# Down projection of a hybrid decoder layer: one block of weights loaded later, from another queue

## The chip, the cores and the metric
The kernel runs on one core of one Trainium2 chip. The metric is the device time of one execution in microseconds (us); the median of three timed executions stands for a kernel. A separate execution is recorded by the hardware profiler, and its trace gives every row below.

The engines are named as the profile names them: PE (TensorE, the matrix engine), PEld (its weight loads), DVE (VectorE), ACT (ScalarE), POOL (GpSimd) and SP (SyncE, which here only issues DMAs). Each engine works through its own instructions in order and waits at one until what it needs is there. DMAs are issued by SP, by POOL or by ACT; "SPq" and "POOLq" are the issues in the profile.

## The reference
One decoder layer in float32 on 512 tokens of width 1024: RMSNorm, attention heads of two kinds, an output projection, then RMSNorm, SwiGLU and a last RMSNorm with a gain:

```
h = h + mix @ w_out
hn = rms_norm(h, norm2_g)
h = h + (silu(hn @ w_gate) * (hn @ w_up)) @ w_down      # w_down: 2816 x 1024
return rms_norm(h, norm_f_g)
```

The change touches only how the product with `w_down` gets its weights.

## The kernel before
All matrix products are made in three passes on a high and a low part of each operand, so that float32 accuracy is kept: `hi*hi + hi*lo + lo*hi`. For each operand ACT makes the high part (a cast, line 70) and DVE the low part (a subtraction, line 75).

**The stages.** Attention and the output projection come first, then the SwiGLU units (22 units of 128 hidden columns), and at the end the down projection, from about 545 us on. The stage before it leaves the hidden activations `zs` in SBUF.

**The down projection** multiplies (512 x 2816) by (2816 x 1024). Rows of tokens, hidden columns and output columns are each cut in half, which gives blocks A11 to A22 of activations and B11 to B22 of weights, and the eight block products are replaced by seven products of sums of blocks (Strassen's scheme in Winograd's form). Here `rows_w(kh, ch, ...)` names a block of weights: kh = 1 is the lower half, ch = 1 the right half. Each product runs over 11 tiles of 128 hidden rows, taken in pairs: six steps, the last with one tile. So there are 42 steps (`steps`, line 909), numbered (n, k) in the code with n from 0; the text counts products from one, so the third product is n = 2.

One step (lines 935 to 955) does the following in order:
- `prepare(n, k)`: the activations are split by ACT (`xe`) and DVE (`xf`), then the weights by ACT (`hl`) and DVE (`hl`, which the profile also writes `hl<-raw,hl`). The split weights have three buffers, the activations four.
- the functions in the fifth field of the product's row in `products`. They change the blocks in place for a later product: `s1` to `s4` change activations on DVE, `t2` and `t3` change weights, and `add_w(kh, ch)` adds a block of weights from DRAM to B11 by accumulating DMAs that POOL issues (line 859).
- `multiply`: for each of two row halves and each tile three matmuls of 512 columns (lines 928 to 930), 12 in a full step, 66 in a product.
- after the third step of a product, the result of the product before is taken from PSUM and added to the output cells in SBUF (`evict`), and after the fourth step `close` squares finished cells on ACT and multiplies those of the left half by the gain `gf` on DVE (`gain`, line 887).

The order of DVE, ACT, POOL and PE within these steps is as written (`tc.manual_schedule`, line 933). The order of SP's loads is written out too (line 823): B11 and B21 (left half), the residual `h1d` into the cells, B22, B12, and last the two halves of `gf`. Outside such blocks a planner orders the instructions by simulated times.

**Where the blocks lie.** B21 takes over buffers that held the transposed input of the SwiGLU units (`x0`), and half of a `raw2` tile; it is read only by the second product. B12 has tiles of its own (`w_hl` and one `w_raw`). In `products` (line 901) the rows that use them are:

```
(ps_b, A12, B21, True, (s1,), ...),               # second product
(ps_a, A21, B11, False, (s4, add_w(1, 0)), ...),  # fourth
(ps_c, A12, B22, False, (t3,), ...),              # fifth
(ps_a, A11, B12, False, (), ...),                 # sixth
(ps_b, A22, B11, True, (), [], [])]               # seventh
```

`t3` adds B22 to B12 before the sixth product reads it. `add_w(1, 0)` in the fourth product adds the lower left block to B11, which the seventh product reads.

Of the kernel before, what the change touches and what calls it, by code (L numbers as in the profile page):

```python
# [11 lines left out]
F32 = mybir.dt.float32  # L12
F32R = mybir.dt.float32r
AF = mybir.ActivationFunctionType
ALU = mybir.AluOpType

P = 128
# [15 lines left out]
WC = 512  # L33
# [4 lines left out]
BUFS = {"w_raw": 3, "w_hl": 5, "pf": 2, "P": 2, "T": 2, "mf": 1, "oc": 1, "g": 3, "h1": 4, "pair": 1, "raw2": 6, "hl2": 3, "xe": 4, "xf": 4}  # L38
# [13 lines left out]
def tile_hybrid_layer(ctx: ExitStack, tc: tile.TileContext, xT, w_qk0, w_t, w_av, w_vb, w_o, w_gu, w_d,  # L52
                      rel, pos2, cw1, cb1, cw2, gT, gf_row, oh, cmask, out):
    nc = tc.nc
# [3 lines left out]
    ws = ctx.enter_context(tc.tile_pool(name="ws", bufs=2))  # L58
# [4 lines left out]
    def bank(tag):  # L63
        return psum.tile([P, 512], F32, name=tag, bufs=BANKS[tag])
# [9 lines left out]
    def tt(e, out, in0, in1, op):  # L74
        engines[e].tensor_tensor(out=out, in0=in0, in1=in1, op=op)  # L75
# [465 lines left out]
    for step in PLAN.split():  # L541
        n, i = step[0], step[1:]
# [34 lines left out]
    def raw2():  # L577
        return ff.tile([P, 2, WC], F32, name="raw2", bufs=BUFS["raw2"])
# [9 lines left out]
    def raw1():  # L588
        return ws.tile([P, WC], F32, name="w_raw", bufs=BUFS["w_raw"])
# [205 lines left out]
    def hidden(half, rows):  # L795

        v = []
        for k in PAIRS:
            j = k.start + (NJ - 10 if k.start < 10 else 1) * rows
            v.append(zq[min(j // 4, 4)][:, j - 4 * min(j // 4, 4):][:, :k.stop - k.start, half * HS:(half + 1) * HS])  # L800
        return v

    A11, A12, A21, A22 = [hidden(h, r) for h in range(2) for r in range(2)]

    def rows_w(kh, ch, n, i):
        k = PAIRS[n].start
        r = k + i + ((NJ - 10 if k < 10 else 1) if kh else 0)
        return w_d[r * P:(r + 1) * P, ch * HD:(ch + 1) * HD]

    def load_w(dst, kh, ch):  # L810
        for n, k in enumerate(PAIRS):
            for i in range(k.stop - k.start):
                nc.sync.dma_start(dst[n][:, i], rows_w(kh, ch, n, i))
# [4 lines left out]
    ps_a, ps_c, ps_b = [[bank(n) for n in tags] for tags in (("PT", "O"), ("S", "S"), ("proj", "proj"))]  # L818
# [4 lines left out]
    with tc.manual_schedule(engines={mybir.EngineType.SP}):  # L823
        r11 = [raw2() for _ in PAIRS]
        B11 = r11[:5] + [r11[5][:, 0:1]]
        load_w(B11, 0, 0)
        x0 = [ff.tile([P, n, WC], F32, name=tag, bufs=1)
              for n, tag in ((4, "X10"), (4, "X11"), (10, "X20"), (10, "X21"))]
        B21 = [x0[k // 2][:, 2 * (k % 2):2 * (k % 2) + 2] for k in range(4)] + [x0[2][:, 8:10], r11[5][:, 1:2]]
        load_w(B21, 1, 0)  # L830
        for t in range(NT):
            nc.sync.dma_start(x0[2][:, 2 * t:2 * t + 2], h1d[t].rearrange("p (c n) -> p c n", c=2))
        B22 = [x0[3][:, 2 * k:2 * k + 2] for k in range(5)] + [raw1()[:, None]]
        load_w(B22, 1, 1)
        B12 = [ws.tile([P, 2, WC], F32, name="w_hl", bufs=BUFS["w_hl"]) for _ in range(5)] + [raw1()[:, None]]
        load_w(B12, 0, 1)
        gf = [ff.tile([P, HD], F32, name="g", bufs=BUFS["g"]) for _ in range(2)]
        for c in range(2):
            nc.sync.dma_start(gf[c], gf_row[:, c * HD:(c + 1) * HD].to_broadcast([P, HD]))
# [16 lines left out]
    def add_w(kh, ch):  # L856
        def f(k):
            for i in range(B11[k].shape[1]):
                nc.gpsimd.dma_start(B11[k][:, i], rows_w(kh, ch, k, i), accum_op=ALU.add)  # L859
        return f  # L860

    def t2(k):
        if k < 4:
            add_w(1, 1)(k)
        else:
            tt("v", B11[k], B11[k], B22[k], ALU.add)

    def t3(k):
        tt("v", B12[k], B12[k], B22[k], ALU.add)

    def evict(ps, th, c, sign=1):

# [21 lines left out]
    def store(t):  # L894
# [7 lines left out]
        (ps_a, A11, B11, True, (s3, add_w(0, 1)), [(ps_a, 0, 0)], []),  # L902
        (ps_b, A12, B21, True, (s1,), [(ps_b, 0, 0)], [(0, 0), (1, 0)]),
        (ps_c, A21, B11, True, (s2, t2), [(ps_c, 1, 1)], []),
        (ps_a, A21, B11, False, (s4, add_w(1, 0)), [(ps_a, 0, 1, -1)], []),
        (ps_c, A12, B22, False, (t3,), [(ps_c, 0, 1)], [(0, 1), (1, 1)]),
        (ps_a, A11, B12, False, (), [(ps_a, 1, 1, -1), (ps_a, 1, 0)], [(2, 1), (3, 1)]),
        (ps_b, A22, B11, True, (), [], [])]
    steps = [(n, k) for n in range(7) for k in range(len(PAIRS))]

# [152 lines left out]
```

## Time and profile before
| | us |
|---|---|
| median of three timed executions | 665.92 (665.73 to 667.33) |
| the profiled execution | 669.47 |
| its span | 667.6 |
| PE busy | 628.0 (94%) |
| DVE busy | 530.5 (79%) |
| ACT busy | 379.5 (57%) |
| POOL busy | 170.0 (25%) |

The span runs from the first to the last instruction of the trace, and the profiled execution's time holds some 2 us around it. Shares of busy time are averages over all stages. A busy PE is not a PE at its peak: matmuls overlap, and their ends are modelled, so their starts are the safer reading.

### The profile page before, as it was taken

The numbers are of one execution on the slowest core, as the hardware profiler recorded it, in microseconds if no ns is written. First come the engines' busy times: TensorE is split into PE (matmuls) and PEld (weight loads), VectorE is DVE, ScalarE is ACT, GpSimd is POOL, SyncE is SP. The second block draws the span as 40 slices with busy tenths as digits, with TensorE's granted clock in tenths as the row PEclk, the third lists the DMA queues.
The fourth block names the chain that finished last, engine by engine and source line by source line (L and its number), as shares of the span: only waits on it lengthen the run. The fifth ranks groups of instructions, "written<-read, shape, count | busy, mean of one in ns | idle before, by whom it ended". The sixth has DMA issues, their size and how long they took to land.

```text
span 667.6 us, 11272 instructions
## 1 busy us (share of the span) xinstructions
PE 628.0 (94%) x3876; PEld 560.3 (84%) x3876; DVE 530.5 (79%) x1072; ACT 379.5 (57%) x785; POOL 170.0 (25%) x214
## 2 busy tenths in 40 slices
PE   9999997989999999987899999999999999859995
PEld 6878887868878888767799999999999988748784
DVE  4558867567787768649899989989999779669995
ACT  4553566245684668747864555555555636615572
POOL 6635852063445555430000000000000040414000
PEclk9999999979999999989899999999999999969998
DMA  5766576346415651043543333233233499949011
GB/s 178 211 189 188 168 182 165 100 132 164 130 36 172 187 192 33 1 163 106 189 141 102 108 127 122 87 111 109 97 113 108 164 258 322 305 85 160 1 63 63
DMA packets 52803, 92.29 MB, mean 138 GB/s; under 512 B 7643, under 2 KB 10971, under 8 KB 52748
## 3 DMA queue, kind: packets, MB, share of 16 engines
q1 hardware_dynamic: 47852, 82.68, 39.3%
q0 software_dynamic: 4320, 7.87, 6.8%
q10 hardware_dynamic: 576, 1.05, 0.4%
q8 instruction: 30, 0.49, 0.3%
q14 instruction: 25, 0.20, 0.1%
HBM read 76.32 MB, written 7.64 MB: 126 GB/s over the span
## 4 chain that ended last, share of the span: by engine, by line
PE 70%; DMA 11%; DVE 9%; ACT 5%; issue 3%; SPq 1%; POOL 1%; ACTq 0%; DVEq 0%; POOLq 0%
PE proj L88 8%; PE proj L90 8%; PE proj L89 8%; PE S L88 6%; PE S L89 6%; PE S L90 6%; PE PT L339 3%; DMA g<-in_gf_dram 2%; DMA X<-h1d 2%; PE S L316 2%; PE O L355 2%; PE O L358 2%; PE S L317 2%; DMA w_raw<-in_w_t_dram 1%; DMA X<-in_w_d_dram 1%
## 5 line engine op out<-in xcount | busy, mean ns | idle before, releaser
L859 POOL DMA_DIRECT2D raw<-in_w_d_dram x30 | 26.5, 1041 | 287.8 <-DVE hl L75 280.8
L70 ACT CAST hl<-raw 128x1024 fp32r<-128x1024 f32 (+1 forms) x69 | 70.5, 1022 | 40.5 <-PE S L930 16.7
L75 DVE TENSOR_TENSOR hl<-raw,hl 128x1024 fp32r<-128x1024 f32 (+1 forms) x69 | 81.2, 1178 | 3.0 <-ACT hl L70 2.9
L70 ACT CAST w_hl<-w_raw 128x512 fp32r<-128x512 f32 (+2 forms) x76 | 43.3, 576 | 63.6 <-PE S L90 19.2
L83 POOL TENSOR_TENSOR w_hl<-w_raw,w_hl 128x512 fp32r<-128x512 f32 (+1 forms) x47 | 61.2, 1306 | 65.2 <-ACT w_hl L70 26.2
L336 POOL TENSOR_SCALAR P<-P,den 128x512 f32<-128x512 f32 (+1 forms) x96 | 51.1, 551 | 39.9 <-DVE den L328 28.1
L324 ACT ACTIVATE P<-P,mn 128x512 f32<-128x512 f32 (+1 forms) x96 | 53.5, 558 | 11.8 <-DVE mn L322 11.5
L75 DVE TENSOR_TENSOR PTl<-PT,PTh 128x512 fp32r<-128x512 f32 (+2 forms) x96 | 43.8, 482 | 10.2 <-ACT PTh L349 9.7
L349 ACT CAST PTh<-PT 128x512 fp32r<-128x512 f32 (+2 forms) x96 | 38.1, 426 | 22.7 <-PE PT L339 18.8
L88 PE MATMUL S<-X,w_hl 128*128 128x256 f32 x176 | 49.9, 284 | 1.0 <-DVE h1t L75 0.5
L88 PE MATMUL S<-X,hl 128*128 128x256 f32 x176 | 50.0, 284 | 0.7 <-ACT xf L724 0.7
L322 DVE CUSTOM_DVE_ANT_0 P<-S,T 128x512 f32<-128x512 f32 (+1 forms) x96 | 43.9, 483 | 8.2 <-PE S L317 6.7
L89 PE MATMUL S<-X,hl 128*128 128x256 f32 x176 | 50.0, 284 | 0.3 <-DVE X L75 0.3
L89 PE MATMUL S<-X,w_hl 128*128 128x256 f32 x176 | 49.8, 283 | 0.0
L90 PE MATMUL S<-X,hl 128*128 128x256 f32 x176 | 49.7, 282 | 0.0
L90 PE MATMUL S<-X,w_hl 128*128 128x256 f32 x176 | 49.6, 283 | 0.0
L88 PE MATMUL proj<-xh,w_hl 128*128 128x512 f32 x112 | 46.1, 412 | 1.2 <-DVE va L281 1.1
L70 ACT CAST w_hl<-raw 128x512 fp32r<-128x512 f32 x45 | 27.3, 620 | 32.3 <-PE S L90 25.7
L90 PE MATMUL proj<-xh,w_hl 128*128 128x512 f32 x112 | 45.6, 407 | 0.0
L89 PE MATMUL proj<-xl,w_hl 128*128 128x512 f32 x112 | 45.4, 406 | 0.0
L83 DVE TENSOR_TENSOR w_hl<-w_raw,w_hl 128x512 fp32r<-128x512 f32 (+1 forms) x37 | 26.1, 710 | 15.0 <-ACT w_hl L70 14.9
L339 PE MATMUL PT<-ident,P 128*128 128x128 f32 x240 | 36.1, 273 | 0.8 <-POOL P L336 0.8
(305 smaller groups left out, 2047.5 us busy)
## 6 DMA issues: line engine op xcount, KB each, us to landing
raw<-in_w_gu_dram SPq DMA_DIRECT2D x46, 256.0 KB, 3.3
w_raw<-in_w_gu_dram SPq DMA_DIRECT2D x42, 256.0 KB, 2.7
raw<-in_w_d_dram POOLq DMA_DIRECT2D x30, 256.0 KB, 8.1
w_raw<-in_w_t_dram SPq DMA_DIRECT2D x28, 256.0 KB, 3.1
X<-in_w_d_dram SPq DMA_DIRECT2D x20, 256.0 KB, 7.5
T<-gd SPq DMA_DIRECT2D x64, 64.0 KB, 2.0
w_raw<-in_w_o_dram SPq DMA_DIRECT2D x16, 256.0 KB, 3.0
raw<-in_w_d_dram SPq DMA_DIRECT2D x12, 256.0 KB, 3.8
```

Source lines behind the costliest of these rows:

```text
L70: nc.scalar.copy(out, in_)
L75: engines[e].tensor_tensor(out=out, in0=in0, in1=in1, op=op)
L83: engines[lo].tensor_tensor(out=w[:, 1, :n], in0=raw[:, :n], in1=w[:, 0, :n].bitcast(F32), op=ALU.subtract)
L88: nc.tensor.matmul(ps, w[:, 0, sl], xh, start=first, stop=False, skip_group_check=skip)
L89: nc.tensor.matmul(ps, w[:, 0, sl], xl, start=False, stop=False, skip_group_check=skip)
L90: nc.tensor.matmul(ps, w[:, 1, sl], xh, start=False, stop=last, skip_group_check=skip)
L322: nc.vector.tensor_tensor_reduce(out=pp, in0=sv, in1=T[:, S - w:], op0=ALU.add, op1=ALU.min, scale=1.0, scalar=3e38, accum_out=mn[:, t:t + 1])
L324: nc.scalar.activation(pp, pp, AF.Exp, bias=mn[:, t:t + 1], scale=-1.0, accum_out=den[:, t:t + 1])
L336: nc.gpsimd.tensor_scalar(pp, pp, den[:, t:t + 1], 1.0, op0=ALU.mult, op1=ALU.mult)
L339: nc.tensor.transpose(pv[:, kb * P:(kb + 1) * P], pp[:, kb * P:(kb + 1) * P], ident)
L349: nc.scalar.copy(ov[0], pv)
L859: nc.gpsimd.dma_start(B11[k][:, i], rows_w(kh, ch, k, i), accum_op=ALU.add)
```

## The change
The upper right block is no longer loaded by SP into tiles of its own. In the fourth product POOL loads it (plain DMAs, the new function `load_12`) over B21, which the second product has read by then. `t3` and the sixth product use B21 in place of B12. The accumulating loads of the lower left block move from the fourth to the fifth product.

```diff
         load_w(B22, 1, 1)
-        B12 = [ws.tile([P, 2, WC], F32, name="w_hl", bufs=BUFS["w_hl"]) for _ in range(5)] + [raw1()[:, None]]
-        load_w(B12, 0, 1)
         gf = [ff.tile([P, HD], F32, name="g", bufs=BUFS["g"]) for _ in range(2)]
...
+    def load_12(k):
+        for i in range(B21[k].shape[1]):
+            nc.gpsimd.dma_start(B21[k][:, i], rows_w(0, 1, k, i))
+
     def t3(k):
-        tt("v", B12[k], B12[k], B22[k], ALU.add)
+        tt("v", B21[k], B21[k], B22[k], ALU.add)
...
-        (ps_a, A21, B11, False, (s4, add_w(1, 0)), [(ps_a, 0, 1, -1)], []),
-        (ps_c, A12, B22, False, (t3,), [(ps_c, 0, 1)], [(0, 1), (1, 1)]),
-        (ps_a, A11, B12, False, (), [(ps_a, 1, 1, -1), (ps_a, 1, 0)], [(2, 1), (3, 1)]),
+        (ps_a, A21, B11, False, (s4, load_12), [(ps_a, 0, 1, -1)], []),
+        (ps_c, A12, B22, False, (t3, add_w(1, 0)), [(ps_c, 0, 1)], [(0, 1), (1, 1)]),
+        (ps_a, A11, B21, False, (), [(ps_a, 1, 1, -1), (ps_a, 1, 0)], [(2, 1), (3, 1)]),
```

## Rows read from the trace of the kernel before

**Rows 1.** The page's 40 equal slices of the span: PE's busy share, in tenths.

```profile
PE   9999997989999999987899999999999999859995
```

**Rows 2.** Waits, 545 to 668 us, then DVE's, 595 to 641: total, times, longest.

```profile
DVE X L75 <- DMA g<-in_gf_dram: 10.5, 1, 10.5
PE S L929 <- DVE hl L75: 10.0, 1, 10.0
...
DVE hl L75 <- ACT hl L70: 0.4, 2, 0.2
```

**Rows 3.** DVE in order of time: start, duration, line, out<-in, [idle before].

```profile
567.29 0.68 DVE L75 TENSOR_TENSOR xf<-act,xe 128x512 fp32r<-128x512 f32 x1
...
576.90 1.22 DVE L75 TENSOR_TENSOR hl<-raw,hl 128x1024 fp32r<-128x1024 f32 x1
...
589.20 1.29 DVE L75 TENSOR_TENSOR X<-X,g 128x512 f32<-128x512 f32 x2 [10.48 <-DMA g<-in_gf_dram]
...
612.11 1.22 DVE L75 TENSOR_TENSOR w_hl<-w_hl,X 128x1024 f32<-128x1024 f32 x1
...
627.59 0.68 DVE L75 TENSOR_TENSOR xf<-act,xe 128x512 fp32r<-128x512 f32 x1
```

**Rows 4.** PE in order of time: products three, six and seven.

```profile
570.97 0.39 PE L928 MATMUL S<-hl,xe 128*128 128x512 f32 x1
...
581.85 0.39 PE L928 MATMUL S<-hl,xe 128*128 128x512 f32 x1
592.28 0.80 PE L929 MATMUL S<-hl,xe 128*128 128x512 f32 x1 [10.04 <-DVE hl L75]
...
629.46 0.50 PE L929 MATMUL PT<-hl,xe 128*128 128x512 f32 x1
...
644.33 0.39 PE L928 MATMUL proj<-hl,xe 128*128 128x512 f32 x1
```

**Rows 5.** Stretches: us, busy PE, PEld, DVE, ACT, POOL; PEclk, DMA, GB/s.

```profile
592.28:597.57 5.29, 5.29 (x12) 4.13 (x13) 5.29 (x9) 0.19 (x1) 0.00 (x0) 0.50 0.00 0
597.88:621.92 24.04, 24.04 (x108) 19.90 (x106) 23.80 (x31) 14.26 (x20) 9.66 (x11) 1.00 0.73 121
```

**Rows 6.** SP's issues in order of time.

```profile
565.84 0.33 SPq L813 DMA_DIRECT2D w_raw<-in_w_d_dram  x1
566.51 6.43 SPq L813 DMA_DIRECT2D w_hl<-in_w_d_dram  x10
...
573.94 1.20 SPq L839 DMA_DIRECT2D g<-in_gf_dram  x2
```

**Rows 7.** DMA by stretch: 552-554, 566-568, 570-573.5, 574-576, 576-578, 596-598.

```profile
raw<-in_w_d_dram POOLq DMA_DIRECT2D x1, 256.0 KB, 13.8
...
q1 hardware_dynamic: 443, 0.81, 105.9%
w_hl<-in_w_d_dram SPq DMA_DIRECT2D x3, 256.0 KB, 5.4
...
w_hl<-in_w_d_dram SPq DMA_DIRECT2D x5, 256.0 KB, 9.5
...
g<-in_gf_dram SPq DMA_DIRECT2D x2, 256.0 KB, 15.7
...
q1 hardware_dynamic: 144, 0.26, 39.7%
...
raw<-in_w_d_dram POOLq DMA_DIRECT2D x1, 256.0 KB, 3.7
```

**Rows 8.** POOL's issues in order of time (duration of the group).

```profile
569.71 1.75 POOL L859 DMA_DIRECT2D raw<-in_w_d_dram  x2 [17.33 <-DVE hl L75]
...
578.42 1.75 POOL L859 DMA_DIRECT2D raw<-in_w_d_dram  x2 [1.74 <-DVE hl L75]
597.88 1.75 POOL L859 DMA_DIRECT2D raw<-in_w_d_dram  x2 [17.71 <-DVE hl L75]
...
608.55 2.65 POOL L859 DMA_DIRECT2D raw<-in_w_d_dram  x3 [0.59 <-DVE hl L75]
```

## The prediction

> **What bounds the kernel now.** I read the 40 slices first. TensorE (PE) is busy 9 tenths nearly everywhere, but slices 35 and 36 of the row (568 to 601 us) fall to 8 and 5 [rows 1]; slice 40 is the tail. This is the down projection, the only stage that the diff touches, so everything below is read there. The list of waits names the stop: VectorE (DVE) waits once, 10.5 us, for the final gain `gf` to be loaded, and PE waits once, 10.0 us, for DVE's `hl` [rows 2]. In DVE's order of time the instruction that waits is the multiplication by the gain (`gain`, line 887), which starts at 589.20 after work that ended at 578.72 [rows 3]. It stands in the fourth step of the third product, in front of `hl` of the fifth step, which PE's second matmul of that step needs: PE starts one matmul at 581.85 and the next at 592.28 [rows 4].
>
> Two things follow. First, PE's clock: after the stop, from 592.28 to 597.57, the granted clock was 0.50 (1.2 of 2.4 GHz), and in the stretch from 597.88 it was 1.00 [rows 5]. Second, DVE from the stop on has no slack: from 595 to 641 it waited 0.4 us in all [rows 2]. Its work for products three to five runs from 567.29 to 627.59, 60.3 us, less the stop of 10.48 49.8 us [rows 3]; PE needs 3 x 66 matmuls at 0.2267 us (10.88 us for 48 matmuls, 570.97 to 581.85 [rows 4]) = 44.9 us. So in these three products DVE and not PE sets the pace, and PE's share only looks full because short waits lie inside overlapped matmuls. From the second matmul of product six (629.46) to product seven (644.33) PE needs 14.87 us for 65 matmuls [rows 4], 0.229 each: PE paces there.
>
> Why is `gf` late? SP issues in order. The last load of the lower right weights is issued at 565.84, then come ten loads `w_hl` from 566.51 on and one more (B12, 256 KB each), and `gf` only at 573.94 [rows 6]. It needs 15.7 us to land, since by then the two queues share the engines: SP's moved 144 packets in 576 to 578, against 443 in 566 to 568 [rows 7]. POOL's accumulating loads of the same time (pairs from 569.71 to 580.17, first and last of four [rows 8]) are the other half.
>
> **The change part by part.**
> *Removed from SP: eleven loads, 2.8 MB.* `gf` moves up to the place of the first of them, 566.5. Landing: the three `w_hl` loads issued in 566 to 568 took 5.4 us, those issued from 570 to 573.5 9.5 us, and `gf` itself 15.7 [rows 7]. So it lands between 571.9 and 582.2. I take 5.4, the row of the same moment: what lies ahead in SP's queue is the same lower right block, and POOL issues its first pair only 3.2 us later. DVE would need `gf` when it ends at 578.72; even 9.5 us (576.0) is in time. At the far end the wait would be 582.2 - 578.7 = 3.5 us.
>
> *What this returns.* At 5.4 or 9.5 us the whole stop of 10.48 us goes. DVE's stream from 589.20 on has no hole until 629.4, so all of it moves up by 10.48, and the first `hl` of product six, which releases PE at 629.46, with it. From there PE paces as before, and the tail hangs on product seven. So the term is 10.5 us. PE's own account gives a ceiling only: its second matmul of the stopped step moves from 592.28 to 582.08, 10.2 us; it would also not lose the 12 matmuls at half clock (5.29 - 12 x 0.2267 = 2.6 us) nor the short waits, (644.33 - 592.28) - 215 x 0.2267 - 2.6 = 0.7 us: 13.5 us together. That cannot be had, as DVE needs 4.9 us more than PE in products three to five, and its lead is small: `hl` of the fourth step ends at 578.12, PE needs it at 581.85 - 12 x 0.2267 = 579.13, so 1.0 us. The time at half clock cost nothing before, because PE then waited less for DVE; that is why I do not add the 2.6. What is late next is DVE's `hl`, in short waits of PE that add up to some 49.8 - 44.9 - 1.0 = 3.9 us over products three to five.
>
> *Added to POOL: eleven plain loads `load_12` in the fourth product.* They wait only for the second product's reads of the same tiles, long done, and stand on POOL's queue behind the third product's accumulating loads, which end their issue at 580.17. A pair of issues takes 1.75 us, 0.88 each, so eleven take 9.6 us: 580.2 to 589.8 [rows 8]. No plain load from this queue is in the trace; the accumulating ones landed in 3.7 us with the engines free and 13.8 us with all queues full [rows 7]. The first pair lands between 585.6 and 595.7. Its reader `t3` starts at 612.11 on DVE [rows 3], with the shift at 601.6: hidden with 6 us to spare at the worst end, and later steps gain, as a step of these products takes DVE 49.8 / 18 = 2.8 us and a pair of issues 1.75. I take zero; DVE would pay each us beyond 601.6.
>
> *Moved one product later: the lower left accumulating loads (`add_w(1, 0)`).* Each waits for the reads of product four, as before, and is now also queued behind `load_12`. They were issued from 597.88 to 611.20 [rows 8]; with the shift product four's readers would free the first at 587.4, and POOL comes to it at 589.8. Eleven issues at 0.88 from there could end by 599.4, but the last is held by its reader, near 600.7. Landing at the worst 13.8 us gives 614.5; PE begins product seven at 644.33 [rows 4], with the shift 633.8, and its operands are prepared at most three steps (8 us) ahead, from 625.6. Hidden by 11 us. Nothing else is on POOL in this stage.
>
> *`t3` and the split read another tile.* Same engine, shape and kind of operands, another place in SBUF: 1.22 us for `t3`'s `w_hl<-w_hl,X`, and 1.22 for a split from `raw` [rows 3]. Zero; no row bounds it better, and 0.1 us on each of ten instructions would be 1 us either way. The third product's accumulating loads lose the competition of B12 and land sooner; their readers are not waiting now, so nothing is gained.
>
> *A rule against the change.* POOL issued a pair in 1.75 us at 597.88, as at 569.71 [rows 8], in a stretch in which DVE was busy 23.80 of 24.04 us [rows 5]. The Trainium skill, page "SBUF — State Buffer", section "SBUF: two separate sides", warns that a DMA issued from GpSimd can be starved of descriptors by some VectorE instructions. By that rule `load_12` would appear after DVE stops (the third rival); the rows do not show such a stop beside these instructions.
>
> *Sum.* The profiled execution took 669.47 us with a span of 667.6, 3.55 us above the median of the runs, 665.92. Taking 10.5 off each: span 657.1, profiled 659.0, median 655.4.
>
> **The rivals.**
> *`gf` still lands late (0.09).* For it: both queues share the engines, and it took 15.7 us before. Against it: what made it slow was B12 ahead and eight accumulating loads beside; the first is gone and the second begins later than the new issue. At 15.7 us the wait is 3.5 us, the gain 7.0 and the time 658.9. The Trainium skill, page "DMA: Bandwidth & Descriptors", section "Issuing engines are not separate DMA queues", says that a transfer gains nothing by another issuing engine; that would hold if `load_12` were in flight beside `gf`, but its turn comes at 580.2.
>
> *No change (0.05).* `gf` could be held at its issue by something other than B12, such as the release of its buffer; then it is issued near 574 and DVE waits as before: 665.9. For it: no row names what released that issue. Against: its buffers were last used by the SwiGLU units, which end before the third product. A different order drawn up by the planner in front of the stage could likewise give back some us; its stages are not in the diff, so I fold this in here.
>
> *Slower: `load_12` cannot be issued beside DVE (0.05).* Place: POOL from 580.2. If POOL could not write its transfers while DVE works, they would start when DVE stops at `t3`, 601.6; the first pair would then cost DVE 1.75 us of issue and 3.7 to 13.8 us of landing, 5.5 to 15.6 us. It turns the result from 10.5 us on, that is from a landing of 8.8 us; at the far end 15.6 - 10.5 = 5.1 us slower, 671.0; at the near end 660.4. Against it stand the eleven issues of 597.88 to 611.20 beside a full DVE.
>
> **How the numbers follow.** The forecast, stop gone and DVE pacing, has 0.81, the rivals 0.09, 0.05 and 0.05. Its own spread is from the ceiling (13.5 us, 652.4) to a `gf` that costs one to two us. The range goes from 652.4 to 659.5 and takes in the first rival, leaving out the rest. About 0.3% (2 us) is what a measurement can tell from no change. Faster: 0.81 + 0.09, less a little for a planner that gives it back, and a part of the third rival is still faster: 0.90. Same: 0.05. Slower: 0.05.
>
> **What would show it.** Right: `gf` issued near 566 and landed before 578; no DVE wait for it, or under 1 us; no 10 us hole in PE and no stretch at clock 0.50 in the third product; eleven POOL issues from about 580 to 590; no DVE wait at `t3`; product six's second matmul near 619, product seven near 634. Short PE waits for `hl` in products three and five show that DVE paces. Wrong: DVE waiting at line 887 for more than 3 us, at `t3`, or on ACT's split of the fourth or seventh product for an accumulating load; or a product seven that starts near 634 with a tail longer than 23 us.

## The result and the profile after

The change made the kernel faster, by about as much as forecast.

| | before | after |
|---|---|---|
| median, us | 666.62 | 657.03 (656.30 to 657.83, 4 runs) |
| ratio | 1 | 0.9849, 95% interval 0.9814 to 0.9883 |
| profiled execution, us | 669.47 | 657.83 |
| its span, us | 667.6 | 656.1 |

The ratio is a gain of 10.1 us (7.8 to 12.4) on 666.62; the forecast was 10.5, and 655.4 us for the median. The line numbers below are those of the changed kernel: `gf` is loaded in line 837, and the matmuls are lines 930 to 932.

First the order in time of SP, which answers to [rows 6] (columns as there).

```profile
563.82 0.33 SPq L813 DMA_DIRECT2D w_raw<-in_w_d_dram  x1
564.53 1.01 SPq L837 DMA_DIRECT2D g<-in_gf_dram  x2
```

`gf` now follows the last lower right load at once, 0.7 us later, where it stood 8.1 us later before. It lands in 5.3 us in place of 15.7, at a moment when SP's queue has the engines to itself (the DMA view of 564 to 566 us; first the queue's packets, then the issues; it answers to [rows 7]):

```profile
q1 hardware_dynamic: 445, 0.81, 105.4%
...
g<-in_gf_dram SPq DMA_DIRECT2D x2, 256.0 KB, 5.3
```

DVE's order of time shows what that gives: the first splits of product three, the gain, `t3` of the first step, and the splits at the start of the sixth product, as in [rows 3].

```profile
565.84 0.69 DVE L75 TENSOR_TENSOR xf<-act,xe 128x512 fp32r<-128x512 f32 x1
566.73 1.23 DVE L75 TENSOR_TENSOR hl<-raw,hl 128x1024 fp32r<-128x1024 f32 x1 [0.20 <-ACT hl L70]
...
576.59 0.69 DVE L846 SCALAR_TENSOR_TENSOR act<-h1t,act 128x512 f32<-128x512 f32 x1
577.19 1.29 DVE L75 TENSOR_TENSOR X<-X,g 128x512 f32<-128x512 f32 x2
...
599.77 1.22 DVE L75 TENSOR_TENSOR X<-X,X 128x1024 f32<-128x1024 f32 x1
...
615.26 0.69 DVE L75 TENSOR_TENSOR xf<-act,xe 128x512 fp32r<-128x512 f32 x1
615.86 1.22 DVE L75 TENSOR_TENSOR hl<-X,hl 128x1024 fp32r<-128x1024 f32 x1
```

The gain carries no idle time, and neither does `t3`. The gain starts 12.01 us earlier than in [rows 3]. Of that, 1.45 us is not the change's: this execution reached product three that much earlier (the split of the activations that starts it is at 565.84, at 567.29 in [rows 3]). In the profile of a kernel below that has the stop again, the down projection is reached earlier than before too (its first `hl` on DVE at 544.24, before 545.88, after 544.43). The rest, 10.56 us, is the stop. By product six the lead is 12.33 us, since a wait of 0.24 us for ACT at the fifth product's start went too. At the end of the span 11.5 us of it are left (667.6 against 656.1): from the start of DVE's last instruction to the end, which is the last stores, it took 5.7 us, 4.9 before. Without the earlier arrival the trace thus shows 10.1 us, as the times do. In the list of waits of DVE from 560 to 640 us one row is left, and PE's own list in the same stretch has two small ones in place of 10.0 us [rows 2]:

```profile
DVE hl L75 <- ACT hl L70: 1.6, 5, 0.7
```

```profile
PE PT L931 <- DVE hl L75: 0.8, 1, 0.8
PE S L931 <- DVE hl L75: 0.6, 1, 0.6
```

PE's order of time shows where these are: the second matmul of products four and six, and one in product five ([rows 4] has the stop and product six).

```profile
584.48 0.39 PE L930 MATMUL PT<-hl,xe 128*128 128x512 f32 x1
585.63 0.49 PE L931 MATMUL PT<-hl,xe 128*128 128x512 f32 x1 [0.76 <-DVE hl L75]
...
608.83 0.39 PE L930 MATMUL S<-hl,xe 128*128 128x512 f32 x1
609.86 0.50 PE L931 MATMUL S<-hl,xe 128*128 128x512 f32 x1 [0.64 <-DVE hl L75]
...
616.71 0.39 PE L930 MATMUL PT<-hl,xe 128*128 128x512 f32 x1
617.14 0.50 PE L931 MATMUL PT<-hl,xe 128*128 128x512 f32 x1
...
632.00 0.39 PE L930 MATMUL proj<-hl,xe 128*128 128x512 f32 x1
```

Where a matmul starts 0.227 us after the one before, nothing waits. Here they start 1.15, 1.03 and 0.43 us after it, so PE lost 0.9, 0.8 and 0.2 us, and the rest in steps of 0.1 us around these places. The starts tell more than the idle time in brackets, which counts from a modelled end. No stretch ran at half clock any more (columns as in [rows 5]; products three to six):

```profile
569.52:632.00 62.48, 61.05 (x265) 49.16 (x264) 61.27 (x85) 38.75 (x60) 21.42 (x29) 1.00 0.63 141
```

62.48 us for 264 matmuls is 2.6 us more than 264 x 0.2267 = 59.85. POOL, last, in order of time (for [rows 8]):

```profile
576.98 1.76 POOL L857 DMA_DIRECT2D raw<-in_w_d_dram  x2 [1.74 <-DVE hl L75]
578.05 4.02 POOL L868 DMA_DIRECT2D X<-in_w_d_dram  x6
582.81 0.54 POOL L868 DMA_DIRECT2D X<-in_w_d_dram  x1 [0.74 <-DMA raw<-in_w_d_dram]
584.75 0.54 POOL L868 DMA_DIRECT2D X<-in_w_d_dram  x1 [1.41 <-DMA X<-in_w_d_dram]
...
587.31 0.54 POOL L868 DMA_DIRECT2D raw<-in_w_d_dram  x1
587.99 3.56 POOL L857 DMA_DIRECT2D raw<-in_w_d_dram  x4
```

The eleven loads of `load_12` (line 868) are issued from 578.05 to 587.85; ten of them, those into `X`, landed in 7.3 us (median). The first is needed at 599.77.

### The profile page after: what moved, and what is told of

The parts are those of the page before. It is cut to its first block, busy times and chain, and to the rows that moved or that the text cites. A ratio compares the mean times of both kernels' runs of the same rounds, so it can differ in the third digit from the quotient of the medians.

```text
span 656.1 us, 11286 instructions
## 1 busy us (share of the span) xinstructions
PE 624.1 (95%) x3876; PEld 557.4 (85%) x3876; DVE 531.7 (81%) x1072; ACT 379.1 (58%) x785; POOL 176.1 (27%) x225
## 4 chain that ended last, share of the span: by engine, by line
PE 68%; DVE 14%; DMA 6%; ACT 4%; issue 4%; POOL 2%; SPq 1%; ACTq 0%; DVEq 0%; POOLq 0%
PE proj L88 7%; PE proj L90 7%; PE proj L89 7%; PE S L88 6%; PE S L89 6%; PE S L90 6%; PE PT L339 3%; PE PT L88 2%; PE PT L89 2%; PE PT L90 2%; DVE hl L75 2%; PE O L355 2%; DVE P L322 2%; PE S L316 1%; PE O L358 1%
```

## The experiments

The theory: all of the gain is that `gf` lands before DVE reaches its multiplication, and the rest of the edit is what must be done with the eleven loads that stood ahead of it. The rivals: the gain comes from fewer bytes in flight beside the transfers that matter, or from where `t3` and the sixth product read. A second question was what bounds the stage now. Each ratio is against runs of the kernel before on the same chip (medians 666.5 to 666.8).

**Only `gf` moved.** The kernel before with the two `gf` loads ahead of B12:

```diff
+        gf = [ff.tile([P, HD], F32, name="g", bufs=BUFS["g"]) for _ in range(2)]
+        for c in range(2):
+            nc.sync.dma_start(gf[c], gf_row[:, c * HD:(c + 1) * HD].to_broadcast([P, HD]))
         B12 = [ws.tile([P, 2, WC], F32, name="w_hl", bufs=BUFS["w_hl"]) for _ in range(5)] + [raw1()[:, None]]
         load_w(B12, 0, 1)
```

> The kernel before with one edit: the two gf loads stand ahead of the eleven B12 loads in SP's order; all else, POOL's order and the tiles too, stays. Theory (the whole gain is that gf lands before DVE reaches line 887): gf is issued near 566 and lands in 5 to 6 us, the 10.5 us wait is gone, about 656 to 658 us, as the changed kernel (657.0). Rival (the gain comes from fewer bytes in flight, or from the tiles and the queue of the upper right block): a wait of several us stays or the time lies clearly above the changed kernel, 660 to 666.

Measured: 655.57 us, ratio 0.9848 (0.9804 to 0.9891). The wait at the gain is gone, `gf` lands in 5.6 us, and PE's two small waits are those of the changed kernel (list of waits of PE, 545 to 640 us):

```profile
PE PT L929 <- DVE hl L75: 0.7, 1, 0.7
PE S L929 <- DVE hl L75: 0.6, 1, 0.6
```

So exchanging the order of `gf` and B12 gives the whole gain, with every byte, tile and queue of the kernel before. ACT waited 3.1 us for accumulating loads here, which it does not do in the changed kernel; PE's waits are not changed by it.

**The loads put back, unread.** The changed kernel with the eleven loads ahead of `gf` again, into tiles that nothing reads:

```diff
+        B12 = [ws.tile([P, 2, WC], F32, name="w_hl", bufs=BUFS["w_hl"]) for _ in range(5)] + [raw1()[:, None]]
+        load_w(B12, 0, 1)
         gf = [ff.tile([P, HD], F32, name="g", bufs=BUFS["g"]) for _ in range(2)]
```

> The changed kernel with the eleven loads of the upper right block put back into SP's order ahead of gf, into tiles of their own that nothing reads; POOL still loads the block that is used. Theory: gf is issued near 574 again, DVE waits about 10 us at the gain, about 666 to 667 us, as before. Rival (the gain lies in where t3 and the sixth product read from, or in POOL's loads): stays near 657.

Measured: 666.22 us, ratio 0.9989 (0.9961 to 1.0017): no gain is left. `gf` is issued at 572.04 and takes 15.4 us, and the list of waits of DVE has the old row again (below SP in order of time):

```profile
572.04 1.02 SPq L839 DMA_DIRECT2D g<-in_gf_dram  x2
```

```profile
DVE X L75 <- DMA g<-in_gf_dram: 9.6, 1, 9.6
```

**Five of them.** The same with five unread loads:

> The changed kernel with five unread loads of 256 KB ahead of gf on SP's queue in place of none (changed) or eleven (the kernel before). Theory (what counts is only whether gf lands before DVE reaches line 887, near 577 us): gf is issued near 567.5 and lands near 576 to 578, a wait of 0 to 1 us, 656.5 to 658 us. Rival (each load ahead of gf costs its share, 10/11 us): 661.5 us.

Measured: 656.55 us, ratio 0.9850 (0.9821 to 0.9878), as the changed kernel beside it (0.9866). The five loads delay `gf` to 568.66 and slow it to 9.1 us (the middle of its two halves; the gain reads only the first), and DVE still does not wait for it (SP, then DVE, in order of time):

```profile
568.66 1.02 SPq L840 DMA_DIRECT2D g<-in_gf_dram  x2
```

```profile
576.98 1.29 DVE L75 TENSOR_TENSOR X<-X,g 128x512 f32<-128x512 f32 x2
```

A share of the gain per load, as the rival has it, would be 661.5 us. With none, five and eleven loads ahead, it is a threshold: five are free, since `gf` is there when DVE comes to it at 577; with eleven it landed near 587 and DVE waited 9.6 us. How steep the cost is between five and eleven was not tried.

**The second half undone.** `add_w(1, 0)` back in the fourth product and `load_12` behind it in the fifth:

```diff
-        (ps_a, A21, B11, False, (s4, load_12), [(ps_a, 0, 1, -1)], []),
-        (ps_c, A12, B22, False, (t3, add_w(1, 0)), [(ps_c, 0, 1)], [(0, 1), (1, 1)]),
+        (ps_a, A21, B11, False, (s4, add_w(1, 0)), [(ps_a, 0, 1, -1)], []),
+        (ps_c, A12, B22, False, (load_12, t3), [(ps_c, 0, 1)], [(0, 1), (1, 1)]),
```

> The changed kernel with the second half of the change undone: add_w(1, 0) is back in the fourth product and load_12 stands in the fifth just ahead of t3, so on POOL's queue it comes behind all eleven accumulating loads of the lower left block. Theory: load_12 is issued only from about 600 us, lands near 607, and DVE waits 7 to 8 us once at t3 of the first step: about 664 to 665 us, so that nearly all of the gain is given back. Rival (the order on POOL's queue doesn't matter, as transfers are hidden anyway): no wait at t3, about 657.

Measured: 664.88 us, ratio 0.9975 (0.9958 to 0.9991). POOL reaches `load_12` at 597.56, and DVE stops once at `t3` (DVE in order of time):

```profile
607.03 1.23 DVE L75 TENSOR_TENSOR X<-X,X 128x1024 f32<-128x1024 f32 x1 [8.23 <-DMA X<-in_w_d_dram]
609.91 1.22 DVE L75 TENSOR_TENSOR X<-X,X 128x1024 f32<-128x1024 f32 x1
```

The wait was forecast at 7 to 8 us and is 8.2; the later steps don't wait. This is the place of the third rival of the prediction, reached by another road: here the load is late because it stands behind accumulating loads that wait for the fourth product, not because POOL could not issue.

**Alternating.** `add_w(1, 0)` back in the fourth product but behind `load_12` of each step:

> The changed kernel with add_w(1, 0) back in the fourth product, but behind load_12 of the same step, so that the two alternate on POOL's queue. Theory (load_12 has 10 us and more to spare): load_12 of each step waits on POOL for the fourth product's reads, lands 4 to 10 us before t3 of its step, no wait at t3: about 657 us, as the changed kernel. Rival (the lower left block had to move by a product for the gain): a wait at t3 in each step, 659 to 662 us.

Measured: 657.08 us, ratio 0.9853 (0.9822 to 0.9885), no wait at `t3`. So the accumulating loads did not have to move by a product; `load_12` only must not stand behind all of them.

**What bounds the stage now.** Four runs took work from DVE. The changed kernel beside the first two:

> The changed kernel once more, as the measure for the three runs beside it. Theory: 656 to 657.5 us, DVE paces products three to five and PE waits for hl some 2.6 us in all from product three to seven, in pieces of about 1 us or less.

Measured: 657.84 us, 0.9866 (0.9834 to 0.9898), with the same waits of PE. Then `t3` by accumulating DMAs in place of DVE additions:

```diff
     def t3(k):
-        tt("v", B21[k], B21[k], B22[k], ALU.add)
+        for i in range(B21[k].shape[1]):
+            nc.gpsimd.dma_start(B21[k][:, i], rows_w(1, 1, k, i), accum_op=ALU.add)
```

> The changed kernel with t3 made by accumulating DMAs on POOL (the lower right block is read once more from DRAM) in place of six DVE additions. DVE has 6.7 us less to do in product five. Theory (DVE paces products three to five after the change): PE's waits in product five and at product six's start go, about 1.4 us, 655 to 656 us; those in product three stay. Rival (PE paces, DVE's work is covered): no change against the changed kernel; a second rival (POOL's queue with eleven more accumulating loads becomes late): a wait at the sixth or seventh product, over 658 us.

Measured: 654.95 us, 0.9825 (0.9795 to 0.9855), 2.9 us under the changed kernel beside it by the medians. The intervals of the two ratios overlap, though the times themselves do not (653.70 to 656.83 here, 656.94 to 658.14 there), so the trace has to show where the gain lies: of the changed kernel's PE waits, those of products five and six are gone, and that of product four stays (PE's waits, 545 to 640 us). From product three to seven PE took 61.06 us against 62.52 in the changed kernel beside it, so 1.5 us are explained, as expected. The two profiled spans differ by 3.1 us (652.7 and 655.8); of the rest, 0.8 us is an earlier start of product three and 0.9 us lies behind the start of product seven, where the stretch to the end takes 22.9 to 24.1 us in the kernels here that have no stop there. So only 1.5 us can be put down to the edit.

```profile
PE PT L932 <- DVE hl L75: 0.8, 1, 0.8
```

Then also the gain of two cells on POOL and the last steps of `t2` by DMA (`k < 6` in `t2`):

```diff
-        tt(ENG["c"], cell(t, 0), cell(t, 0), gf[0], ALU.mult)
+        tt("p" if t < 2 else ENG["c"], cell(t, 0), cell(t, 0), gf[0], ALU.mult)
```

> As the run before, and the last two steps of t2 by accumulating DMAs too, and the gain of the first two cells on POOL: DVE has 3.1 us less in product three as well. Theory: PE runs from product three to seven without waits, 2.6 us less than the changed kernel, 654 to 655 us. Rival (DVE's work is covered): no change, 657 us.

Measured: 659.33 us, 0.9890 (0.9862 to 0.9918): this was a miss. The wait of 0.9 us at the start of product four did go (one of 0.3 us appears later in that product), but the two multiplications on POOL took 6.8 us, 1.29 on DVE, and everything behind them on POOL's queue slipped (POOL in order of time):

```profile
575.62 1.75 POOL L857 DMA_DIRECT2D raw<-in_w_d_dram  x2 [1.74 <-DVE hl L75]
576.72 6.83 POOL L75 TENSOR_TENSOR X<-X,g 128x512 f32<-128x512 f32 x2
```

Its last accumulating load is issued at 618.01; ACT then waited for loads (list of waits of ACT, 545 to 640 us), and PE for ACT at the seventh product:

```profile
ACT hl L70 <- DMA raw<-in_w_d_dram: 4.5, 2, 2.4
ACT hl L70 <- DMA X<-in_w_d_dram: 4.3, 2, 2.2
```

To tell the gain on POOL from the number of accumulating loads, the last two kernels leave the gain on DVE, start from the kernel with `gf` moved ahead of B12 (so POOL has no plain loads), and issue `t3`'s accumulating loads in the fourth product. One has `t2` wholly by DMA, one does not:

```diff
-        if k < 4:
+        if k < 6:
             add_w(1, 1)(k)
...
     def t3(k):
-        tt("v", B12[k], B12[k], B22[k], ALU.add)
+        for i in range(B12[k].shape[1]):
+            nc.gpsimd.dma_start(B12[k][:, i], rows_w(1, 1, k, i), accum_op=ALU.add)
...
-        (ps_a, A21, B11, False, (s4, add_w(1, 0)), [(ps_a, 0, 1, -1)], []),
-        (ps_c, A12, B22, False, (t3,), [(ps_c, 0, 1)], [(0, 1), (1, 1)]),
+        (ps_a, A21, B11, False, (s4, t3, add_w(1, 0)), [(ps_a, 0, 1, -1)], []),
+        (ps_c, A12, B22, False, (), [(ps_c, 0, 1)], [(0, 1), (1, 1)]),
```

> The kernel before with gf ahead of B12 on SP's queue, t3 by accumulating DMAs into B12 in the fourth product and the last two steps of t2 by accumulating DMAs; the gain stays on DVE. POOL then issues 33 accumulating loads and no plain ones. Theory (DVE paces products three to five; in the run with the gain on POOL it was POOL's multiplications and the late adds behind them that took the profit back): PE's waits of product three to six go, about 2.5 us under the changed kernel, 654 to 655 us, with no wait of ACT for a load. Rival (POOL's queue of accumulating loads is the next bound): ACT waits for B11 in the fourth or seventh product, 657 us or more.

> As the run beside it, but t2 is left on DVE in its last two steps. Theory: the wait of 1.1 us at the fourth product's start stays, those of products five and six go, about 1.4 us under the changed kernel and 1 us over the run beside it: 655 to 656 us. Rival: as beside it, no difference between the two.

Measured: 652.82 us, 0.9790 (0.9763 to 0.9817) with `t2` by DMA, the fastest of all kernels here, and 655.65 us, 0.9834 (0.9805 to 0.9863) without. In the first PE has no wait from product three to seven: 264 matmuls in 59.84 us, the 2.6 us of the changed kernel gone. No changed kernel ran beside these two; by the ratios the first lies 4 to 5 us under it, of which the trace shows these 2.6.

```profile
568.02:627.86 59.84, 59.84 (x266) 49.57 (x264) 53.71 (x77) 38.88 (x60) 27.49 (x32) 1.00 0.98 210
```

In the second the wait of 0.9 us in product four is the main one left, as in the run with `t3` alone, and PE takes 61.08 us: 1.24 us between the two, as forecast, where the medians differ by 2.8. Accumulating loads, 33 on POOL's queue, were not the bound; ACT waited 1.7 us for them in all, against the forecast of none, without reaching PE. So what spoiled the miss was what else stood on POOL's queue. The trace of the miss names the two multiplications (6.8 us, and the last load was issued 8.6 us later than in the run with `t3` alone, with three accumulating loads more); no run here takes only them off POOL, so the shares of the multiplications and of the loads are not shown. Both kernels differ from the changed one also in the order of `gf` and B12; the first experiment says that this alone leaves the time as it is.

## Why the prediction was right

**The bound and the term.** The stop at the gain was the whole case: forecast 10.48 us, found 10.56 in the trace and 10.1 (7.8 to 12.4) in the times. The median was forecast at 655.4 and is 657.03: 0.7 us of the difference is that the kernel before has 666.62 with one more run in its median, the rest is within the interval. The experiment with `gf` alone shows that this one wait was it; the unread loads bring it back.

**The landing of `gf`.** Taken at 5.4 us from the loads issued at the same moment, measured 5.3. The middle value, 9.5 us, was tried by the five unread loads (9.1 us, no wait), so the choice between it and 5.4 did not matter. The far value, 15.7 us at the early issue, was in no run: with the eleven loads `gf` took 15.4 us, but its issue was late as well. Against that value, the operation's own row, the row of the same moment decided 3.5 us of the sum.

**DVE paces.** It was the reason to take 10.5 and not PE's ceiling of 13.5. From product three to seven PE's time fell from 73.36 us [rows 4] to 62.48, which is the stop and 0.4 us; the 2.6 us at half clock did not come back on top, as the prediction said. The kernel with `t2` and `t3` taken off DVE shows the difference: the 2.6 us of PE's waits are then had as well. One number in this step was off: PE's remaining waits were put at 3.9 us, in products three and five, and they were 2.6, at the starts of products four and six and in product five. The step set DVE's excess over three products (4.9 us) against its lead at the fourth step (1.0), and counted that lead to the step's first matmul, though the low part of `hl` is read by the second. In the changed kernel, counted from `hl` to `hl`: DVE ends the first one of product three at 567.96 and the first one of product six at 617.08, 49.1 us; PE needs 198 x 0.2267 = 44.9 us between the second matmuls of the same steps; and the lead at the start is 1.8 us (PE's second matmul is at 569.75). So 49.1 - 44.9 - 1.8 = 2.4 us must be waits, and the second matmul of product six, at 617.14, is 2.5 us later than it would be without any. The sum did not use the 3.9.

**The added loads.** Forecast from 580.2 to 589.8, hence with the 1.45 us of the earlier arrival 578.7 to 588.3; found from 578.05 to 587.85. The working was right by luck in part: a plain load has an issue of 0.54 us here, not in the 0.88 of an accumulating one, but POOL was held up to 1.4 us at some of them by DMAs still in flight. The margin to `t3` was real, and so was its price: the run with the load behind the accumulating ones paid 8.2 us of wait.

**The rivals.** `gf` late by the shared engines did not happen: when it was issued, only SP's own queue moved data (445 packets in 564 to 566 us, none from POOL). That something else held its issue (the second rival) did not happen, as it follows the load ahead of it by 0.7 us. That POOL could not issue beside a busy DVE did not happen either: DVE was busy all of the 9.80 us from 578.05 to 587.85 in which `load_12` was issued. The near end of that rival should read 660.9 us, not 660.4 (655.4 + 5.5). The rule of the Trainium skill named in the prediction, page "SBUF — State Buffer", section "SBUF: two separate sides", speaks of two-port instructions of VectorE; no run here has shown one beside a DMA issue. But POOL's multiplications with two SBUF operands did collide, see below.

**The signs.** With the earlier arrival of 1.45 us added, `gf` was issued at 566.0, product six's second matmul came at 618.6 and product seven at 633.5, all as forecast (566, 619, 634). One sign of being wrong was there by its words, a product seven near 634 with a tail longer than 23 us: the tail was 24.1 us. But it was set too tight, as the kernel before already has 23.3 (644.33 to 667.6); the 0.8 us between them lie in the last stores and come and go between kernels with the same end (23.1 us with the five unread loads).

**What the change did not need.** Neither the move of the load to POOL nor that of the accumulating loads brings time; they do no harm. Exchanging the order of `gf` and B12 on SP's queue does the same.

## What to carry to other kernels

Where an engine waits for a load, look at what its queue issued ahead of it and when each of these is needed: an order in which the load that is needed first goes first cost nothing here and gave 10 us. Before adding up what a vanished stop returns, find which engine has no slack behind it; the return here was that engine's stop (10.5 us), not all that the busiest engine lost around it in idle time, half clock and short waits (13.5 us). And a load that is moved to another in-order queue is as late as what stands in front of it there: behind loads that wait for compute it gave back 8 of 10 us.

## What the runs showed of the hardware

Two multiplications of 128x512 with both operands in SBUF took 6.83 us on POOL beside a busy DVE (4.58 and 2.28; another POOL product of that form took 1.28 elsewhere in the run), against 1.29 us for both on DVE; and DVE suffered too (DVE in order of time in that run, where the same forms take 1.22 and 0.69 us otherwise):

```profile
578.51 0.69 DVE L75 TENSOR_TENSOR hl<-raw,hl 128x512 fp32r<-128x512 f32 x1
...
580.34 2.05 DVE L75 TENSOR_TENSOR hl<-raw,hl 128x1024 fp32r<-128x1024 f32 x1 [0.20 <-ACT hl L70]
582.31 1.79 DVE L75 TENSOR_TENSOR act<-act,act 128x512 f32<-128x512 f32 x1
```

The Trainium skill, page "SBUF — State Buffer", section "Who interferes with whom", says that a VectorE instruction with two SBUF inputs contends with a GpSimd instruction that reads SBUF; this trace agrees in part, with 0.8 and 1.1 us lost on two DVE instructions. The six DVE instructions that started from 576.44 to 579.45 kept their length, though by the profile POOL's first multiplication began at 576.72; the profile's spans on POOL are rough, and no run here tells how much of its 6.83 us was work.

In the same run PE's clock fell after two waits close together at the seventh product, where matmuls started 1.44 and 1.25 us apart: the stretch from 629.00 to 635.10 had a mean granted clock of 0.72, with matmuls 0.43 us apart in it as at the 0.50 of [rows 5]. The changed kernel's single waits, with starts 1.15 us apart and less, left it at 1.00.

In the fastest kernel the accumulating DMAs carried 33 loads of 256 KB from 567 to 610 us, the first of them beside SP's plain ones, without PE waiting once: adding a block of weights on its way from DRAM cost less here than six DVE additions (61.06 us from product three to seven against 62.52, the run with `t3` alone), though it reads the block a second time.
